# A two-layer trunk with a top-2-of-8 MoE: the last half in a fixed order, with a fourth pair of split buffers

## The chip, the cores and the metric

The kernel runs on one core of one Trainium2 chip. The metric is the device time of one execution in microseconds (us); it is compared as the median of several runs. The kernel before takes 1392.92 us (three runs, 1392.0 to 1393.23). Engines are called PE (TensorE, with its weight loads as PEld), DVE (VectorE), ACT (ScalarE), POOL (GpSimd) and SP (the engine that issues the DMAs).

## The reference

Input x has 256 tokens of 1024 values. There are two layers; each is a gated token mixer with four branches, then a feed-forward part: a dense SwiGLU in layer 0, a mixture of 8 SwiGLU experts in layer 1. The change lies in the experts alone:

```python
def swiglu(t, w1, w3, w2):
    return (jax.nn.silu(t @ w1) * (t @ w3)) @ w2

logits = t @ router
top_vals, top_idx = lax.top_k(logits, 2)
weights = jax.nn.softmax(top_vals, axis=-1)
combine = jnp.sum(jax.nn.one_hot(top_idx, 8) * weights[..., None], axis=1)
out = sum(combine[:, e:e + 1] * swiglu(t, w1[e], w3[e], w2[e]) for e in range(8))
```

Each expert has w1 and w3 of 1024 x 2816 and w2 of 2816 x 1024, all float32, 34.6 MB in sum. A final RMSNorm follows.

## The kernel before

**Precision.** A float32 matrix is split into two float32r parts: hi, a rounded copy made by ACT (`split_hi`, L132), and lo, the rest, made by DVE (`lo_parts`, L152). Products are summed in PSUM from hi x hi, lo x hi and hi x lo.

**The weight stream.** `plan` lists all weight tiles in the order of their use. A tile is 128 x 2048 float32, 1 MiB (the two last are half as large). `WeightStream` keeps three counters: tiles loaded, split hi, split lo. `SLOTS` names, for each phase of the plan, the SBUF slots that may hold a raw tile, a hi part or a lo part. `load` (L116, on SP) issues the next load once a raw slot is free, that is once DVE has made the lo part of the tile that was in it; `get` hands out a tile and splits ahead as far as slots are free.

**The experts.** The router's counts are ranked, and the four busiest experts get 128 slots each, the other four (`LIGHT`) 64 slots each (`Q`). An expert is worked through in six steps, chunks of 512 columns of the 2816 (the last has 256). A step of a full chunk uses two tiles of w1, two of w3, and two of w2 for the chunk before: six tiles. An expert has 33 tiles.

In the 64-slot half, the hi and lo part of the tokens stand side by side as 128 columns of one stationary operand, so that a weight tile costs eight matmuls of 512 columns: four with its hi part, then four with its lo part (`both`, L558). The banks of w1 and w3 are copied out by ACT (g and gb, L1314), the two halves of 64 are added by a short matmul with a folding matrix (L1352, `folded`), then ACT makes SiLU (L1355), DVE the product (L1356), ACT its hi part (L438) and DVE its lo part (L439). The result is the stationary operand of the w2 tiles, which are summed over the six chunks in two banks (yps). After an expert's last w2 tile these are weighted and split (y, L441 and L442), and after two experts matmuls with the slot masks (put) scatter them back to the tokens, which DVE adds to x (`scatter`, L1419 and L1420). The last expert's last chunk has its own function (`last_down`). Then the final norm is computed and written out.

**What sets the order.** The kernel is written in the order of the data. Where nothing else is said, a planner sets the order of each engine's instructions as it builds the program, by modelled times and free buffers. Some stretches (`manual_schedule`: the transitions between parts, and the routing) are in the order of the text; the loop over expert steps in `experts` is not one of them. Each engine, and SP's queue, carries out its instructions strictly in the order set.

Raw, hi and lo slots: while the first three steps with 64 slots per expert are used, 9 raw, 3 hi and 3 lo (phase moe2); then 11 raw (moe3), from step `M2` on 10 (moe and end), always with 3 hi and 3 lo.

Of the kernel before, what the change touches and what calls it, by code (L numbers as in the profile page):

```python
# [8 lines left out]
F32 = mybir.dt.float32  # L9
# [46 lines left out]
M0, M1, MQ, M2, END = 6, 11, 27, 40, 47  # L56
LIGHT, Q = 4, 64
FT = DFF // P
# [8 lines left out]
class WeightStream:  # L67
# [6 lines left out]
    def __init__(self, tc, plan, slots):  # L74
        self.tc, self.nc, self.plan, self.slots = tc, tc.nc, plan, slots
        self.gate = []
        self.pools, self.owner = {}, {}
        self.last_pair = {n: j for j, t in enumerate(plan) for kind in ("hi", "lo") for n in slots[t[-1]][kind]}
# [8 lines left out]
    def take(self, kind, j, dt):  # L87
        free = []
        for slot in self.slots[self.plan[j][-1]][kind]:
            if slot not in self.pools or (kind == "raw" and self.last_pair.get(slot, -1) >= self.nlo):  # L90
# [82 lines left out]
    def split_all(self, upto, parts):  # L173
        while self.nlo < min(upto, len(self.plan)):
            if not ((self.nhi > self.nlo or self.split_hi()) and self.split_lo(parts)):
                return

# [26 lines left out]
class Trunk:  # L204
# [56 lines left out]
    def plan(self):  # L261
# [19 lines left out]
        for l in self.layers:  # L281
# [27 lines left out]
            else:  # L309
                steps = [(e, c) for e in range(NE) for c in range(len(CHUNKS))]  # L310
                for s in range(len(steps) + 1):
                    phase = "late" if s == 0 else "moe0" if s < M0 else "moe1" if s < M1 else "moe2" if s < MQ else "moe3" if s < M2 else "moe" if s < END else "end"
# [21 lines left out]
    def spread_gain(self, src, row, out):  # L334

        nc = self.nc
        nc.vector.memset(row[0:1, D : D + P], 1.0)
        nc.sync.dma_start(row[0:1, :D], src[None, :])
        banks = [self.acc("gainps") for _ in range(2)]
        for c, ps in enumerate(banks):  # L340
            nc.tensor.matmul(ps, row[0:1, D : D + P], row[0:1, c * 512 : (c + 1) * 512], start=True, stop=True)
        for c, ps in enumerate(banks):
            nc.scalar.activation(out[:, c * 512 : (c + 1) * 512], ps, AF.Copy)
# [864 lines left out]
    def experts(self, l, ep, ap, xp, tok, cw, pos, pick, g0):  # L1208
# [51 lines left out]
        def place(pair):  # L1260

            ps = self.acc("putps")
            for j in range(2):
                for t in range(NT):
                    nc.tensor.transpose(
                        ps[:, j * T + t * P : j * T + (t + 1) * P], mask(t, pair, j).bitcast(F32), self.ident
                    )
            put = ep.tile([P, 2, T], F32R, tag="put", name="put")
# [3 lines left out]
        def weigh(pair):  # L1272

            ps = self.acc("wslps")
            for j in range(2):
                for t in range(NT):
                    nc.tensor.matmul(
                        ps[:, 2 * j : 2 * j + 2], mask(t, pair, j), cw2[:, t, 2 * pair + j, :], start=t == 0, stop=t == NT - 1
                    )
            nc.vector.tensor_reduce(  # L1280
# [3 lines left out]
        for s in range(1, len(steps)):  # L1284
            if s < len(steps):
                e, c = steps[s]
                c0, n = CHUNKS[c]
                nk = 2048 // n
                heavy = e < LIGHT
                xv = xe[e // 2] if heavy else xe["both"]  # L1290
                outs = []
                for nm in ("w1", "w3"):
                    ps = self.mm(nm)
                    nt = NK // nk
                    for k0 in range(nt):
                        w = ws.get((nm, l, e, c, k0))
                        if heavy:
                            self.prod(
                                ps[:, :n], lambda i, k: xv[i][:, k0 * nk + k, e % 2, :], lambda j, k: w[j][:, k, :],
                                range(nk), start=k0 == 0, stop=k0 == nt - 1,  # L1300
                            )
                        else:
                            self.both(
                                ps[:, :n], lambda k: xv[:, k0 * nk + k, e - LIGHT, :], lambda j, k: w[j][:, k, :],
                                range(nk), start=k0 == 0, stop=k0 == nt - 1,
                            )
                    outs.append(ps)
                if heavy:
                    g = self.gate(ep, *outs, n)
                else:  # L1310
                    sums = []
                    for ps, tag in zip(outs, ("g", "gb")):
                        half = ep.tile([P, 512], F32, tag=tag, name=tag)
                        nc.scalar.activation(half[:, :n], ps[:, :n], AF.Copy)  # L1314
                        sums.append(half)
            if len(done) == 2 or done and done[0][0] == NE - 2:
                self.scatter(done, put)
                done = []
            if s == M2 + 2:
                row = self.extra.tile([P, 2 * D], F32, tag="u", name="gain")  # L1320
                self.gain = row[:, D:]
                self.spread_gain(self.a["final_norm"], row, self.gain)
# [6 lines left out]
            if s < len(steps):  # L1329
                nf = n // P  # L1330
                ps = self.mm("actps")
                if heavy:
                    for f in range(nf):
                        nc.tensor.transpose(ps[:, f * P : (f + 1) * P], g[:, f * P : (f + 1) * P], self.ident)
                    act = act_pair()
                    self.hilo(*(x[:, :nf, :] for x in act), ps[:, :n].rearrange("p (f s) -> p f s", f=nf))
                else:
                    act = self.folded(ep, ap, ps, sums, nf)
                acts[s] = act
                if e in (1, 3) and c < 4:  # L1340
                    if c == 0:
                        pick = self.picks(ep, pos, e // 2 + 1)
                    gather(e // 2 + 1, c)
        self.last_down(l, acts, ys[NE - 1], wsl, put)

    def folded(self, ep, ap, ps, sums, nf):

        nc = self.nc
        for j, x in enumerate(sums):
            for f in range(nf):  # L1350
                o = j * T + f * Q
                nc.tensor.matmul(ps[:, o : o + Q], x[:, f * P : (f + 1) * P], self.fold, start=True, stop=True)  # L1352
        n = nf * Q
        g = ep.tile([P, T], F32, tag="gf", name="gf")
        nc.scalar.activation(g[:, :n], ps[:, :n], AF.Silu)  # L1355
        nc.vector.tensor_tensor(g[:, :n], ps[:, T : T + n], g[:, :n], op=ALU.mult)  # L1356
        act = ap.tile([P, 4, P], F32R, tag="ah", name="act", bufs=2)
        self.hilo(act[:, :nf, :Q], act[:, :nf, Q:], g[:, :n].rearrange("p (f s) -> p f s", f=nf))
        return act
# [50 lines left out]
    def scatter(self, done, put):  # L1410

        nc = self.nc
        for t in range(NT):
            for half in range(2):
                s = slice(half * 512, (half + 1) * 512)
                ps = self.acc("scps")
                parts = [(e, y) for e, pair in done for y in pair]
                for n, (e, y) in enumerate(parts):
                    nc.tensor.matmul(ps, put[:, e % 2, t * P : (t + 1) * P], y[:, s], start=n == 0, stop=n == len(parts) - 1)  # L1419
                nc.vector.tensor_tensor(self.x[t][:, s], self.x[t][:, s], ps, op=ALU.add)  # L1420
# [150 lines left out]
```

## Time and profile before

| | us |
|---|---|
| median of three runs | 1392.92 |
| the profiled execution | 1393.16 |
| its span, first to last instruction | 1391.2 |
| busy in the span: PE | 1315.8 |
| DVE | 1057.4 |
| ACT | 869.0 |
| HBM read | 384.99 MB, 277 GB/s over the span |

The span runs from the first to the last instruction on the core; the execution takes 1.96 us more. An engine's busy time is the time in which at least one of its instructions runs; matmuls are pipelined, so that a busy PE need not be at its peak. "DMA share" is the mean busy share of the 16 DMA engines. A wait is put down to what came last before the instruction started. The first 64-slot tile is used at about 1004 us.

### The profile page before, as it was taken

The page shows a single profiled execution, that of the slowest core. Times are in us where ns is not written, and L with a number is a line of the kernel's source. Part 1 is how long each engine was busy: PE and PEld are TensorE (multiplying, and loading weights), DVE is VectorE, ACT ScalarE, POOL GpSimd, SP SyncE. Part 2 cuts the span into 40 slices and gives each one's busy share as a digit, 9 for nine tenths or more (in the row PEclk, how much of TensorE's full clock was granted, in tenths as well). Part 3 has the DMA queues.
Part 4 walks back from the last instruction along what each step waited for, and adds up shares of the span by engine and source line. Part 5 has one row for each costly group of instructions (what it writes and reads, how often), then busy time and mean ns, then how long its engine had stood idle before and what let it go on. Part 6 is the DMA issues. An engine that isn't in the chain of part 4 may idle for free. (4 is left out here: it accounts for less than half of the span.)

```text
span 1391.2 us, 20094 instructions
## 1 busy us (share of the span) xinstructions
PE 1315.8 (95%) x8088; PEld 1149.6 (83%) x8088; DVE 1057.4 (76%) x874; ACT 869.0 (62%) x775; POOL 30.0 (2%) x52
## 2 busy tenths in 40 slices
PE   6999999999999999999999999999999888988885
PEld 6999999999989999978888888888877666666653
DVE  5976666554467766678888898888899888987986
ACT  5644445433455444457776776777788867777774
POOL 3110000000000000000000000000000000000000
PEclk9999999999999999999999999999999999999998
DMA  8746556565545676658989899999999999999980
GB/s 277 247 133 219 191 181 219 177 194 182 182 159 190 210 280 206 213 198 297 345 310 343 323 357 340 371 353 353 354 400 407 412 388 366 361 353 362 350 302 31
DMA packets 212127, 387.40 MB, mean 278 GB/s; under 512 B 7791, under 2 KB 98733, under 8 KB 212030
## 3 DMA queue, kind: packets, MB, share of 16 engines
q1 hardware_dynamic: 211214, 383.90, 77.6%
q0 software_dynamic: 816, 2.17, 0.5%
q8 instruction: 65, 1.06, 0.3%
q14 instruction: 32, 0.26, 0.0%
HBM read 384.99 MB, written 1.05 MB: 277 GB/s over the span
## 5 line engine op out<-in xcount | busy, mean ns | idle before, releaser
L152 DVE TENSOR_TENSOR J<-B,F 128x2048 fp32r<-128x2048 f32 x27 | 61.8, 2290 | 36.6 <-ACT F L132 35.4
L152 DVE TENSOR_TENSOR I<-A,E 128x2048 fp32r<-128x2048 f32 (+1 forms) x28 | 62.0, 2214 | 30.7 <-ACT E L132 30.7
L132 ACT ACTIVATE F<-B 128x2048 fp32r<-128x2048 f32 x27 | 51.7, 1913 | 39.0 <-PE mm L552 14.8
L839 ACT ACTIVATE sg<-mm,cols 128x256 f32<-128x256 f32 x64 | 26.8, 470 | 77.8 <-PE mm L552 49.7
L132 ACT ACTIVATE E<-A 128x2048 fp32r<-128x2048 f32 (+1 forms) x28 | 51.9, 1853 | 36.1 <-issue 12.6
L152 DVE TENSOR_TENSOR K<-C,G 128x2048 fp32r<-128x2048 f32 x25 | 57.2, 2290 | 16.8 <-ACT G L132 16.7
L152 DVE TENSOR_TENSOR L<-D,H 128x2048 fp32r<-128x2048 f32 x20 | 45.8, 2290 | 24.3 <-ACT H L132 24.3
L132 ACT ACTIVATE G<-C 128x2048 fp32r<-128x2048 f32 x25 | 47.8, 1913 | 25.5 <-issue 11.7
L558 PE MATMUL w<-I,xe 128*128 128x512 f32 (+1 forms) x176 | 47.6, 396 | 16.9 <-DVE I L152 16.9
L558 PEld LDWEIGHTS w<-I,xe 128*128 128x128 f32 x176 | 29.8, 195 | 29.7 <-DVE I L152 25.7
L132 ACT ACTIVATE H<-D 128x2048 fp32r<-128x2048 f32 x20 | 38.3, 1917 | 25.3 <-PE mm L552 11.1
L558 PE MATMUL w<-E,xe 128*128 128x512 f32 (+1 forms) x176 | 44.5, 378 | 0.7 <-ACT E L132 0.7
L152 DVE TENSOR_TENSOR K<-B,G 128x2048 fp32r<-128x2048 f32 (+1 forms) x17 | 35.7, 2102 | 8.5 <-ACT G L132 7.9
L845 DVE TENSOR_TENSOR sg<-pr,sg 128x512 f32<-128x512 f32 x24 | 16.6, 692 | 33.2 <-ACT sg L839 33.2
L450 POOL TENSOR_TENSOR rstd<-rstd,mhalf 128x1 f32<-128x1 f32 (+1 forms) x14 | 12.5, 895 | 1322.5 <-ACT fo L455 780.8
L152 DVE TENSOR_TENSOR J<-A,F 128x2048 fp32r<-128x2048 f32 (+1 forms) x17 | 35.6, 2100 | 6.2 <-ACT F L132 6.2
L558 PE MATMUL w<-J,xe 128*128 128x512 f32 (+1 forms) x128 | 32.7, 381 | 7.9 <-DVE J L152 7.8
L152 DVE TENSOR_TENSOR J<-t,F 128x2048 fp32r<-128x2048 f32 x15 | 34.4, 2290 | 7.2 <-ACT F L132 6.8
L152 DVE TENSOR_TENSOR K<-H,G 128x2048 fp32r<-128x2048 f32 x15 | 34.4, 2290 | 7.0 <-ACT G L132 6.9
L552 PE MATMUL w<-E,xe 128*128 128x512 f32 (+1 forms) x168 | 38.9, 372 | 0.0
L152 DVE TENSOR_TENSOR I<-s,E 128x2048 fp32r<-128x2048 f32 (+1 forms) x16 | 34.4, 2155 | 4.9 <-ACT E L132 4.8
L152 DVE TENSOR_TENSOR K<-D,G 128x2048 fp32r<-128x2048 f32 (+1 forms) x16 | 34.4, 2155 | 4.6 <-ACT G L132 4.6
(565 smaller groups left out, 3981.0 us busy)
## 6 DMA issues: line engine op xcount, KB each, us to landing
B<-in_moe_w_dram SPq DMA_DIRECT2D x26, 1024.0 KB, 6.5
C<-in_moe_w_dram SPq DMA_DIRECT2D x26, 1024.0 KB, 6.0
D<-in_moe_w_dram SPq DMA_DIRECT2D x26, 1024.0 KB, 6.4
s<-in_moe_w_dram SPq DMA_DIRECT2D x26, 1024.0 KB, 7.0
A<-in_moe_w_dram SPq DMA_DIRECT2D x25, 1024.0 KB, 6.8
H<-in_moe_w_dram SPq DMA_DIRECT2D x25, 1024.0 KB, 5.7
L<-in_moe_w_dram SPq DMA_DIRECT2D x25, 1024.0 KB, 5.9
t<-in_moe_w_dram SPq DMA_DIRECT2D x25, 1024.0 KB, 6.6
```

Of the source, the lines that this page charges most:

```text
L132: self.nc.scalar.activation(t[:, s], self.raw[j][:, s], AF.Copy)
L152: self.nc.vector.tensor_tensor(t[:, s], self.raw[j][:, s], self.hi[j][:, s].bitcast(F32), op=ALU.subtract)
L450: self.power = nc.gpsimd.tensor_tensor(r, t, self.mhalf[:, :n], op=ALU.pow)
L552: nc.tensor.matmul(ps, lhs(i, k), rhs(j, k), start=start and n == 0, stop=stop and n == len(steps) - 1)
L558: self.nc.tensor.matmul(ps, lhs(k), rhs(j, k), start=start and n == 0, stop=stop and n == len(steps) - 1)
L839: nc.scalar.activation(sg[:, s], psg[:, s], AF.Sigmoid, bias=self.col(l, "b_gate", i * 8 + 2 * j + c))
L845: nc.vector.tensor_tensor(sg, pr[j], sg, op=ALU.mult)
```

## The change

The phases of the 64-slot half get other slots: raw slots H and L become a fourth hi and a fourth lo slot. A slot may hold raw tiles until the plan needs it as part of a pair (`pair_due`). The loop over steps ends at the 128-slot half; the 64-slot half is a new function, `light`, which runs inside `manual_schedule` for ACT, DVE and PE. It walks through the tiles of the plan. For tile i it writes PE's matmuls, then PE's other work that is due, then the hi split of tile i+4, then ACT's other work that is due, then the lo split of tile i+2, then DVE's other work that is due. "Due" is given by `at(kind, j, f)`: f stands behind PE's tile j, behind the hi split of tile j, or behind the lo split of tile j. The work itself (copies, folds, SiLU, products, splits, scatters) is as before.

```diff
-    "moe3": {"raw": "ABCDHLstuyz", "hi": "EFG", "lo": "IJK"},
-    "end": {"raw": "ABCDHLstyz", "hi": "EFG", "lo": "IJK"},
-    "moe": {"raw": "ABCDHLstyz", "hi": "EFG", "lo": "IJK"},
+    "moe3": {"raw": "ABCDstu", "hi": "EFGH", "lo": "IJKL"},
+    "moe4": {"raw": "ABCDstuyz", "hi": "EFGH", "lo": "IJKL"},
+    "moe5": {"raw": "ABCDstyz", "hi": "EFGH", "lo": "IJKL"},
+    "end": {"raw": "ABCDstyz", "hi": "EFGH", "lo": "IJKL"},
...
-M0, M1, MQ, M2, END = 6, 11, 27, 40, 47
+M0, M1, ML, MQ, M2, END = 6, 11, 24, 27, 40, 47
+PHASES = ((1, "late"), (M0, "moe0"), (M1, "moe1"), (ML, "moe2"), (MQ, "moe3"), (M2, "moe4"), (END, "moe5"), (99, "end"))
+AHEAD_HI, AHEAD_LO = 4, 2
...
+    def pair_due(self, slot, j):
+        at = self.pair_at.get(slot, ())
+        n = bisect_left(at, self.nlo)
+        return n < len(at) and at[n] < j
...
+    def ahead(self, nhi, nlo):
+        while self.nhi < min(nhi, len(self.plan)):
+            assert self.split_hi()
+        while self.nlo < min(nlo, len(self.plan)):
+            assert self.split_lo()
...
+        ws.release()
+        with self.tc.manual_schedule(engines={ACT, DVE, PE}):
+            self.light(l, ep, ap, xe["both"], acts, ys, done, wsl, masks, place_parts)
+        self.last_down(l, acts, ys[NE - 1], wsl, masks["put"])
...
+        def up(i, w, nm, e, c, k0):
...
+            self.both(
+                ps[:, :n], lambda k: x4[:, k0 * nk + k, e - LIGHT, :], lambda j, k: w[j][:, k, :],
+                range(nk), start=k0 == 0, stop=last,
+            )
+            if nm == "w1" and k0 == 0:
+                if s % 12 == PLACE:
+                    turn, put, find, put_weights = place_parts(s // 12)
+                    at("mm", i + 1, turn)
+                    at("hi", i + 5, put)
+                    at("mm", i + 2, find)
+                    at("lo", i + 4, put_weights)
...
+            at("hi", i + 4, copy)
+            if nm == "w1":
+                return
...
+            if s == NE * len(CHUNKS) - 1:
+                for f in (fold, silu, mult, act_hi, act_lo):
+                    at("mm", i + 1, f)
+                return
+            at("mm", i + 2, fold)
+            at("hi", i + 6, silu)
+            at("lo", i + 4, mult)
+            at("hi", i + 7, act_hi)
+            at("lo", i + 5, act_lo)
+
+        def down(i, w, e, c, k0):
...
+            at("hi", i + 4, y_hi)
+            at("lo", i + 3, y_lo)
...
+            for t in range(NT):
+                at("mm", i + 3 + t, lambda t=t: scatter(t))
+                at("lo", i + 5 + t, lambda t=t: self.add_scattered(t, sums[t]))
+
+        first = ws.nuse
+        ws.ahead(first + AHEAD_HI, first + AHEAD_LO)
+        for i in range(first, len(ws.plan) - len(LAST)):
+            key, w = ws.hand_out()
+            if key[0] == "w2":
+                down(i, w, *key[2:])
+            else:
+                up(i, w, key[0], *key[2:])
+            ws.release()
+            run("mm", i)
+            ws.ahead(i + 1 + AHEAD_HI, 0)
+            run("hi", i + AHEAD_HI)
+            ws.ahead(0, i + 1 + AHEAD_LO)
+            run("lo", i + AHEAD_LO)
```

`copy`, `fold`, `silu`, `mult`, `act_hi`, `act_lo`, `y_hi`, `y_lo` and `scatter` hold one instruction, or one loop of them, of the list in the section before. The load of the final norm's gain and its spreading are cut in two in the same manner.

## Rows read from the trace of the kernel before

**Rows 1.** The page's sums: busy us (share of the span) and instructions per engine.

```profile
PE 1315.8 (95%) x8088; PEld 1149.6 (83%) x8088; DVE 1057.4 (76%) x874; ACT 869.0 (62%) x775; POOL 30.0 (2%) x52
```

**Rows 2.** Stretches: from:to, length, busy PE, PEld, DVE, ACT, POOL; clock, DMA share, GB/s.

```profile
650.00:1004.00 354.00, 354.00 (x1713) 296.31 (x1712) 310.13 (x186) 258.12 (x180) 0.00 (x0) 1.00 0.95 346
1004.00:1023.00 19.00, 19.00 (x94) 15.85 (x93) 18.96 (x12) 19.00 (x16) 0.00 (x0) 1.00 0.99 371
1020.00:1130.00 110.00, 97.90 (x481) 77.22 (x481) 99.18 (x66) 86.27 (x74) 0.00 (x0) 1.00 1.04 410
1130.00:1350.00 220.00, 188.31 (x888) 141.34 (x888) 187.37 (x119) 167.58 (x140) 0.00 (x0) 0.99 0.99 361
1004.00:1376.00 372.00, 324.33 (x1550) 248.68 (x1549) 322.94 (x213) 287.20 (x249) 0.00 (x0) 0.99 0.94 350
```

**Rows 3.** Waits of the engines, 1004 to 1376: us in total, times, longest us.

```profile
ACT g L1314 <- PE w L558: 27.5, 19, 2.0
...
DVE I L152 <- ACT E L132: 18.9, 15, 1.5
...
DVE I L152 <- DMA z<-in_moe_w_dram: 0.2, 1, 0.2
```

**Rows 4.** Order of time within 1150 to 1200: start, length, instruction [idle before, releaser].

```profile
1155.09 2.28 DVE L152 TENSOR_TENSOR J<-D,F 128x2048 fp32r<-128x2048 f32 x1
...
1155.92 1.08 PE L558 MATMUL w<-F,xe 128*128 128x512 f32 x4
1157.29 2.29 DVE L152 TENSOR_TENSOR K<-s,G 128x2048 fp32r<-128x2048 f32 x1
...
1158.66 0.60 ACT L1314 ACTIVATE g<-w 128x512 f32<-128x512 f32 x1 [1.96 <-PE w L558]
1159.15 1.90 ACT L132 ACTIVATE E<-A 128x2048 fp32r<-128x2048 f32 x1
...
1159.38 1.04 PE L1352 MATMUL actps<-fold,g 128*128 128x64 f32 x8
...
1161.09 2.29 DVE L152 TENSOR_TENSOR I<-A,E 128x2048 fp32r<-128x2048 f32 x1 [1.52 <-ACT E L132]
...
1163.44 1.19 PE L558 MATMUL w<-I,xe 128*128 128x512 f32 x4 [1.11 <-DVE I L152]
```

**Rows 5.** Waits of the DMA queue on SP, 1004 to 1376.

```profile
SPq L116 <- DVE gf L1356: 56.1, 20, 3.6
```

**Rows 6.** DMA, 1020 to 1130: packets, MB, share; issues, KB each, median us to landing.

```profile
q1 hardware_dynamic: 19829, 44.97, 104.1%
...
y<-in_moe_w_dram SPq DMA_DIRECT2D x4, 1024.0 KB, 11.4
z<-in_moe_w_dram SPq DMA_DIRECT2D x4, 1024.0 KB, 9.3
```

**Rows 7.** DMA, 1004 to 1376.

```profile
q1 hardware_dynamic: 58576, 130.00, 93.6%
...
B<-in_moe_w_dram SPq DMA_DIRECT2D x1, 512.0 KB, 4.7
```

**Rows 8.** Order of time at the end.

```profile
1346.64 0.38 SPq L116 DMA_DIRECT2D B<-in_moe_w_dram  x1
...
1364.68 0.39 ACT L1314 ACTIVATE gb<-w 128x256 f32<-128x256 f32 x1 [0.33 <-PE w L558]
...
1366.86 0.27 ACT L1355 ACTIVATE gf<-actps 128x128 f32<-128x128 f32 x1
...
1368.05 1.15 ACT L132 ACTIVATE G<-B 128x512 fp32r<-128x512 f32 x2
1368.32 0.28 DVE L1356 TENSOR_TENSOR gf<-actps,gf 128x128 f32<-128x128 f32 x1
...
1369.09 0.30 ACT L438 ACTIVATE act<-gf 128x128 fp32r<-128x128 f32 x1
...
1370.93 0.28 DVE L439 TENSOR_TENSOR act<-gf,act 128x128 fp32r<-128x128 f32 x1
```

More of the change, by code (lines that the diff above doesn't have):

```diff
@@ L1 @@
+from bisect import bisect_left
 from contextlib import ExitStack, contextmanager
@@ L77, in __init__ @@
         self.pools, self.owner = {}, {}
-        self.last_pair = {n: j for j, t in enumerate(plan) for kind in ("hi", "lo") for n in slots[t[-1]][kind]}
+        self.pair_at = {}
+        for j, t in enumerate(plan):
+            for n in slots[t[-1]]["hi"] + slots[t[-1]]["lo"]:
+                self.pair_at.setdefault(n, []).append(j)
         self.raw, self.hi, self.lo = {}, {}, {}
@@ L89, in take @@
         for slot in self.slots[self.plan[j][-1]][kind]:
-            if slot not in self.pools or (kind == "raw" and self.last_pair.get(slot, -1) >= self.nlo):
+            if slot not in self.pools or (kind == "raw" and self.pair_due(slot, j)):
                 continue
@@ L176, in split_all, with hand_out @@
                 return
+    def ahead(self, nhi, nlo):
[3 more added lines that the diff above has]
+            assert self.split_lo()
+    def hand_out(self):
+        i = self.nuse
+        assert self.nlo > i
+        key, _, k, c, _ = self.plan[i]
+        self.nuse += 1
+        return key, tuple(t.pop(i)[:, : k * c].rearrange("p (k c) -> p k c", k=k) for t in (self.hi, self.lo))
     def get_many(self, keys, ahead=True):
@@ L311, in plan @@
                 for s in range(len(steps) + 1):
-                    phase = "late" if s == 0 else "moe0" if s < M0 else "moe1" if s < M1 else "moe2" if s < MQ else "moe3" if s < M2 else "moe" if s < END else "end"
+                    phase = next(name for end, name in PHASES if s < end)
                     if s < len(steps):
@@ L332, in bcast, with load_row, spread_row, copy_row @@
         (eng or self.nc.gpsimd).dma_start(t, bass.AP(tensor=src.tensor, offset=src.offset, ap=[[0, P], [1, n]]))
[L334 to L338, printed above, removed]
+    def load_row(self, src, row):
+        self.nc.vector.memset(row[0:1, D : D + P], 1.0)
+        self.nc.sync.dma_start(row[0:1, :D], src[None, :])
+    def spread_row(self, row):
         banks = [self.acc("gainps") for _ in range(2)]
         for c, ps in enumerate(banks):
-            nc.tensor.matmul(ps, row[0:1, D : D + P], row[0:1, c * 512 : (c + 1) * 512], start=True, stop=True)
+            self.nc.tensor.matmul(ps, row[0:1, D : D + P], row[0:1, c * 512 : (c + 1) * 512], start=True, stop=True)
+        return banks
+    def copy_row(self, banks, out):
         for c, ps in enumerate(banks):
-            nc.scalar.activation(out[:, c * 512 : (c + 1) * 512], ps, AF.Copy)
+            self.nc.scalar.activation(out[:, c * 512 : (c + 1) * 512], ps, AF.Copy)
     def load_gain(self, src, eng=None):
@@ L1282, in weigh @@
             )
[L1284 to L1316, printed above, removed]
@@ new lines, in experts @@
+        for s in range(1, ML):
+            e, c = steps[s]
+            c0, n = CHUNKS[c]
+            nk = 2048 // n
+            xv = xe[e // 2]
+            outs = []
+            for nm in ("w1", "w3"):
+                ps = self.mm(nm)
+                nt = NK // nk
+                for k0 in range(nt):
+                    w = ws.get((nm, l, e, c, k0))
+                    self.prod(
+                        ps[:, :n], lambda i, k: xv[i][:, k0 * nk + k, e % 2, :], lambda j, k: w[j][:, k, :],
+                        range(nk), start=k0 == 0, stop=k0 == nt - 1,
+                    )
+                outs.append(ps)
+            g = self.gate(ep, *outs, n)
+            if len(done) == 2:
@@ L1317, in experts @@
                 self.scatter(done, put)
                 done = []
[L1319 to L1322, printed above, removed]
             if s % 12 == PLACE:
@@ L1328, in experts @@
                 done.append((steps[s - 1][0], y))
[L1329 to L1332, printed above, removed]
-                    for f in range(nf):
[L1334 to L1359, printed above, removed]
+            nf = n // P
@@ new lines, in experts @@
+            ps = self.mm("actps")
+            for f in range(nf):
+                nc.tensor.transpose(ps[:, f * P : (f + 1) * P], g[:, f * P : (f + 1) * P], self.ident)
+            act = act_pair()
+            self.hilo(*(x[:, :nf, :] for x in act), ps[:, :n].rearrange("p (f s) -> p f s", f=nf))
+            acts[s] = act
+            if e in (1, 3) and c < 4:
+                if c == 0:
+                    pick = self.picks(ep, pos, e // 2 + 1)
+                gather(e // 2 + 1, c)
+        masks = {"put": put}
@@ new lines, in place_parts, with put @@
+        def place_parts(pair):
+            def put():
+                masks["put"] = put_masks(masks["ps"])
+            return (
+                lambda: masks.update(ps=turn_masks(pair)), put,
+                lambda: masks.update(wps=find_weights(pair)), lambda: set_weights(pair, masks["wps"]),
+            )
+        ws.release()
+        with self.tc.manual_schedule(engines={ACT, DVE, PE}):
+            self.light(l, ep, ap, xe["both"], acts, ys, done, wsl, masks, place_parts)
+        self.last_down(l, acts, ys[NE - 1], wsl, masks["put"])
@@ new lines, in light, with at, run, copy @@
+    def light(self, l, ep, ap, x4, acts, ys, done, wsl, masks, place_parts):
+        nc, ws = self.nc, self.ws
+        todo = {"mm": [], "hi": [], "lo": []}
+        bank, half, now = {}, {}, [0]
+        def at(kind, j, f):
+            todo[kind].append((j, len(todo[kind]), f))
+        def run(kind, upto):
+            ready = sorted((x for x in todo[kind] if x[0] <= upto), key=lambda x: x[:2])
+            todo[kind] = [x for x in todo[kind] if x[0] > upto] if len(ready) < len(todo[kind]) else []
+            for _, _, f in ready:
+                f()
+        def up(i, w, nm, e, c, k0):
+            c0, n = CHUNKS[c]
+            nk, s = 2048 // n, e * len(CHUNKS) + c
+            if k0 == 0:
+                bank[nm] = self.mm(nm)
+            ps = bank[nm]
+            last = k0 == NK // nk - 1
+            self.both(
+                ps[:, :n], lambda k: x4[:, k0 * nk + k, e - LIGHT, :], lambda j, k: w[j][:, k, :],
+                range(nk), start=k0 == 0, stop=last,
+            )
+            if nm == "w1" and k0 == 0:
[5 more added lines that the diff above has]
+                    at("lo", i + 4, put_weights)
+                if s == M2 + 2:
+                    row = self.extra.tile([P, 2 * D], F32, tag="u", name="gain")
+                    self.gain = row[:, D:]
+                    banks = []
+                    self.load_row(self.a["final_norm"], row)
+                    at("mm", i + 6, lambda: banks.extend(self.spread_row(row)))
+                    at("hi", i + 10, lambda: self.copy_row(banks, self.gain))
+            if not last:
+                return
+            def copy():
+                half[nm] = ep.tile([P, 512], F32, tag={"w1": "g", "w3": "gb"}[nm], name="half")
+                nc.scalar.activation(half[nm][:, :n], ps[:, :n], AF.Copy)
+            at("hi", i + 4, copy)
+            if nm == "w1":
+                return
+            nf, box = n // P, {}
+            def fold():
+                box["ps"] = out = self.mm("actps")
+                for j, x in enumerate((half["w1"], half["w3"])):
+                    for f in range(nf):
+                        o = j * T + f * Q
+                        nc.tensor.matmul(out[:, o : o + Q], x[:, f * P : (f + 1) * P], self.fold, start=True, stop=True)
+            m = nf * Q
+            def silu():
+                box["g"] = ep.tile([P, T], F32, tag="gf", name="gf")
+                nc.scalar.activation(box["g"][:, :m], box["ps"][:, :m], AF.Silu)
+            def mult():
+                nc.vector.tensor_tensor(box["g"][:, :m], box["ps"][:, T : T + m], box["g"][:, :m], op=ALU.mult)
+            def act_hi():
+                acts[s] = act = ap.tile([P, 4, P], F32R, tag="ah", name="act", bufs=2)
+                nc.scalar.activation(act[:, :nf, :Q], box["g"][:, :m].rearrange("p (f s) -> p f s", f=nf), AF.Copy)
+            def act_lo():
+                act = acts[s]
+                nc.vector.tensor_tensor(
+                    act[:, :nf, Q:], box["g"][:, :m].rearrange("p (f s) -> p f s", f=nf), act[:, :nf, :Q].bitcast(F32),
+                    op=ALU.subtract,
+                )
+            if s == NE * len(CHUNKS) - 1:
+                for f in (fold, silu, mult, act_hi, act_lo):
+                    at("mm", i + 1, f)
+                return
+            at("mm", i + 2, fold)
[4 more added lines that the diff above has]
+        def down(i, w, e, c, k0):
+            if c == 0 and k0 == 0:
+                ys[e] = [self.acc("yps") for _ in range(2)]
+            y, act = ys[e], acts[e * len(CHUNKS) + c]
+            n = CHUNKS[c][1]
+            last = c == len(CHUNKS) - 1 and k0 == n // 256 - 1
+            for h in range(2):
+                self.down_part(
+                    e, y[h], act, k0, lambda j, k: w[j][:, k, h * 512 : (h + 1) * 512], c == 0 and k0 == 0, last,
+                )
+            if k0 == n // 256 - 1:
+                del acts[e * len(CHUNKS) + c]
+            if not last:
+                return
+            halves = [slice(h * 512, (h + 1) * 512) for h in range(2)]
+            weight = wsl[:, e : e + 1]
+            def y_hi():
+                pair = self.extra.tile([P, 2, D], F32R, tag="wx"[e % 2], name="y")
+                done.append((e, (pair[:, 0], pair[:, 1])))
+                for s, ps in zip(halves, y):
+                    nc.scalar.activation(pair[:, 0, s], ps, AF.Copy, scale=weight)
+            def y_lo():
+                hi, lo = done[-1][1]
+                for s, ps in zip(halves, y):
+                    nc.vector.scalar_tensor_tensor(
+                        lo[:, s], ps, weight, hi[:, s].bitcast(F32), op0=ALU.mult, op1=ALU.subtract
+                    )
+            at("hi", i + 4, y_hi)
+            at("lo", i + 3, y_lo)
+            if e % 2 == 0 and e < NE - 2:
+                return
+            sums = {}
+            def scatter(t):
+                sums[t] = self.scatter_half(done, masks["put"], t)
+                if t == NT - 1:
+                    done.clear()
+            for t in range(NT):
[15 more added lines that the diff above has]
+            run("lo", i + AHEAD_LO)
+        for kind in todo:
+            run(kind, 10**9)
@@ L1410, in scatter, with scatter_half, add_scattered @@
     def scatter(self, done, put):
-        nc = self.nc
         for t in range(NT):
[L1414 to L1420, printed above, removed]
+            self.add_scattered(t, self.scatter_half(done, put, t))
+    def scatter_half(self, done, put, t):
+        banks = []
+        for half in range(2):
+            s = slice(half * 512, (half + 1) * 512)
+            ps = self.acc("scps")
+            parts = [(e, y) for e, pair in done for y in pair]
+            for n, (e, y) in enumerate(parts):
+                self.nc.tensor.matmul(
+                    ps, put[:, e % 2, t * P : (t + 1) * P], y[:, s], start=n == 0, stop=n == len(parts) - 1
+                )
+            banks.append(ps)
+        return banks
+    def add_scattered(self, t, banks):
+        for half, ps in enumerate(banks):
+            s = slice(half * 512, (half + 1) * 512)
+            self.nc.vector.tensor_tensor(self.x[t][:, s], self.x[t][:, s], ps, op=ALU.add)
     def overflow(self, l, th, tl, cw, pos, cnti):
```

8 lines of the change are left out of this document (added).

## The prediction

> **What bounds the kernel now.** I read the sums of the page first, then the busy times by stage, then the waits of the last stage, then its instructions in order of time, then the DMA queue.
>
> The sums [rows 1] name no bound: TensorE (PE) 95%, VectorE (DVE) 76%. By stage [rows 2] there are two. From 650 to 1004 us, the experts with 128 slots, PE is busy 354.00 of 354.00 us: that half is bound by PE and the change doesn't touch it. From 1004 us on, the experts with 64 slots, no engine is full: over 1130:1350 PE has 188.31 of 220 us, DVE 187.37, ScalarE (ACT) 167.58, at 361 GB/s. One weight tile is 1 MiB (1.0486 MB), so 361 GB/s x 220 us is 79.4 MB or 75.7 tiles, and a tile takes 2.90 us, of which PE is busy 2.49, DVE 2.48, ACT 2.21. Busy counts the tails of waiting matmuls, so these are upper bounds of the work.
>
> Why a tile takes 2.90 us is in the waits [rows 3] and in the order of time [rows 4]. Nothing waits for data: DVE waited 0.2 us for a DMA, once. Instead the three engines wait for each other in a ring. At 1158.66 ACT copies a finished bank (g) after 1.96 us idle, because the bank needs PE's last matmuls; the hi split of the next tile (E from A) is queued behind that copy and starts at 1159.15; DVE's lo split of that tile waits for it, 1.52 us idle, to 1161.09; PE waits for that lo, 1.11 us idle, to 1163.44; and the next copy waits for PE. This happens at the g copy and at the gb copy, twice in every step of six tiles. With three hi and three lo buffers no engine is far enough ahead to cover it.
>
> The DMA queue follows this ring. SP waits for DVE to free a raw buffer, for some 260 us of 372 in five such lines, the longest of them in [rows 5]. Where more buffers were free, 1020:1130, the same loads ran at 410 GB/s with the 16 engines' packets at 104.1% of the time and 9.3 to 11.4 us from issue to landing [rows 2, 6]: by the rate 2.557 us a tile, so some four tiles in flight. That is the DMA's own limit as far as this trace shows it, and it lies above the 2.48 to 2.49 us of DVE and PE.
>
> **The change, part by part.**
> *Instructions.* None is added or removed: the same splits, matmuls, folds, copies and sums, in another order. Cost 0.
>
> *The fixed order.* The hi split of tile i+4 and the lo split of tile i+2 now stand ahead of PE's tile i+1, and each copy, SiLU and product stands behind a split that comes later. I followed one step through the order with DVE as the bound (DVE splits start 2.20 us apart, [rows 4]; PE 0.91 us for half a tile, estimated from its 1.08 us less the tail; ACT 1.90 a split). Say DVE ends the lo of the second tile after w3 at 0. PE ends that tile at 1.0 and the fold (16 short matmuls, 1.04 us for eight in [rows 4]) at about 2.9; ACT's SiLU ends at 3.3; DVE wants it at 4.4, after two more splits. The product ends at 4.8, ACT's next hi split (it needs PE's first half of the tile after the fold) at 5.7, act hi at 6.1; DVE wants it at 7.0. So both meeting points have about 1 us in hand, and the ring is gone. ACT needs 6 x 1.90 plus 2 us in a step of over 14. What is late next is the load: 2.557 us a tile against 2.48.
>
> *When the load is the bound*, ACT's hi split starts as a tile lands; the same order makes DVE wait for ACT to be two tiles ahead (product and act lo), so a raw buffer is freed up to some 7.5 us after landing (two tiles of 2.56, and a lo split). This costs nothing as long as enough loads are in flight.
>
> *Raw buffers.* Two become a hi and a lo slot: before 10 (11 and 9 at the edges), after 7 for the first three steps, then 9, then 8. A buffer's round is landing time plus the time it is held: 8 x 2.557 = 20.5 us, less 7.5 held, leaves 13 us, more than the 9.3 to 11.4 us that a saturated landing took [rows 6]. With 7 it leaves 10.4, just enough. Bounds: nothing, or the rate of a queue that runs shallow (346 GB/s over 650:1004, [rows 2]). I take the upper rate, 410, since the held time is nearer to that case. But two fewer tiles are in the buffers when the stage starts (7 for 9): 2 x 2.557 = +5.1 us; bounds 0 and 5.1.
>
> *The end.* Now the last load is issued at 1346.64 and lands 4.7 us later, at 1351.3 [rows 7, 8], 39.9 us before the end, because landed tiles are queued in the buffers. A stage bound by loads has no such queue. After the last landing comes its hi split 1.15, the copy behind it 0.39, fold (eight short matmuls) 1.04, SiLU 0.27, product 0.28, act hi 0.30, act lo 0.28 [rows 4, 8], six hand-overs at an estimated 0.15, together 4.6; from act lo's end (1371.2) to the end of the span are 20.0 us today; the last two lo splits now stand behind act lo, an estimated +0.4. Sum 25.0, bounds 22 and 39.9.
>
> *A rule against it.* In 1020:1130 the loads ran at 410 GB/s [rows 2, 6]. The Trainium skill, "DMA: Bandwidth & Descriptors", section "Where 436 GB/s comes from", says that for HBM to SBUF the limit of HBM per core, about 358 GB/s, binds. By it the loads could not speed up over today's 361, and the estimate of the stage would be 130.00 / 0.358 = 363 us. The trace disagrees for 110 us on end with one core running, but its last 220 us do stand near that figure, so it is a rival below.
>
> **The sum**, on the profiled execution:
> - start of the stage 1004, unchanged
> - loads left at 1004: 130.00 MB [rows 7]; the first 19 us as now, 371 GB/s [rows 2], 7.05 MB; the other 122.95 MB at 410 GB/s: 299.9 us; last landing 1322.9
> - two tiles less in the buffers: 1328.0
> - the end: 1353.0
> - for stalls I can't place (a scatter of 16 matmuls twice in the stage, seven buffers at its start) 1% of 300 us, my estimate: 1356.0, a span shorter by 35.2 us
> - outside the span 1393.16 - 1391.2 = 1.96; the median 1392.92 lies 0.24 under the profiled run: 1357.7.
>
> **The rivals.**
> 1. *Forecast*: loads bind, 1358 (own range 1350 to 1366). 0.62.
> 2. *The order stalls at places of its own.* In-order engines now have each small operation nailed behind a split; if the 1 us in hand is used up by hand-overs or by landings that vary, DVE's idle time comes back in part. It is 372 - 322.94 = 49 us now [rows 2]; half of it on top of the floor of rival 3: 1372. 0.17.
> 3. *Loads faster than I think, DVE binds.* DVE's busy time from 1004 to its act lo, 322.94 less some 2 us after it, ends at 1325; plus 20.0 and 1.7: 1347. Against it: 104.1% at 410 GB/s. 0.08.
> 4. *The loads stay at today's late rate*, 361 GB/s: 130.00 / 0.361 = 360.1 us from 1004; with or without the two tiles (5.8) and with the end of 25.0 and 1.7: 1391 to 1397. For it: packets already at 99% of the time over 1130:1350 [rows 2]. Against: SP waits for DVE there, and the same packets' share stood at 95% with 346. 0.06. By the skill's 358 it would be 1394 to 1400.
> 5. *Slower: too few raw buffers.* A buffer that is held longer than 20.5 - 10.4 = 10.1 us past its landing (7.5 in the first three steps) lets the queue run shallow. Place: every lo split that waits behind a product or act lo. Price: at the 346 GB/s of [rows 2], 130.00 / 0.346 = 375.7, two tiles 6.1, end 25.0, 1.7: 1412. Against it: my 7.5 us. 0.07.
>
> That the change doesn't do what it says I hold for excluded: nothing but the order and the slots is left to go wrong.
>
> **How the numbers follow.** About 0.2% (2.8 us) is what a measurement here tells from no change. Forecast and rivals 2 and 3 are faster: 0.87. Rival 4 is split, 0.03 the same and 0.03 slower; with rival 5 slower is 0.10. The range 1346 to 1378 holds the forecast, rival 3 and most of rival 2, about 0.83.
>
> **What would show it.** Right: SP no longer waits for DVE most of the time; DVE and ACT wait for DMA landings; about 405 to 415 GB/s from 1030 to 1320; the last landing near 1328 and 25 us to the end; ACT's idle time before the g and gb copies (27.5 us for g alone, [rows 3]) gone. Rival 2: DVE waits for ACT or PE with landed tiles in hand. Rival 3: over 420 GB/s. Rivals 4 and 5: waits for data at 346 to 361 GB/s, rival 4 with landings over 10 us, rival 5 with short landings and SP waiting for DVE before each issue. I am wrong in the first step if the half before 1004 us moves.

## The result, and the profile after

The changed kernel takes 1355.99 us (median of four runs, 1354.36 to 1356.61), the kernel before 1392.84 us beside it: a ratio of 0.9734, 95% interval 0.9718 to 0.9751. The forecast was 1357.7 us. The profiled execution is the shortest of the four, 1354.36 us with a span of 1352.7 us, 38.5 us less than before.

The stretches of the changed kernel come first: from:to, length, then busy PE, PEld, DVE, ACT, POOL; granted clock, DMA share, GB/s.

```profile
650.00:1004.00 354.00, 354.00 (x1714) 296.31 (x1713) 312.82 (x188) 261.14 (x182) 0.00 (x0) 1.00 0.94 340
1004.00:1023.00 19.00, 19.00 (x93) 15.87 (x92) 16.42 (x12) 17.56 (x16) 0.00 (x0) 1.00 1.05 408
1020.00:1130.00 110.00, 104.02 (x508) 84.07 (x507) 106.29 (x68) 94.72 (x78) 0.00 (x0) 0.97 1.04 409
1130.00:1310.00 180.00, 168.38 (x817) 132.90 (x815) 170.98 (x111) 155.27 (x129) 0.00 (x0) 0.99 1.05 410
1004.00:1337.00 333.00, 313.27 (x1535) 250.84 (x1533) 314.95 (x209) 284.22 (x245) 0.00 (x0) 0.98 1.01 396
```

Against [rows 2], the 128-slot half has the same busy PE, and the 64-slot half now moves 410 GB/s to its end, where it had fallen to 361. DVE went from 322.94 busy of 372 us (87%) to 314.95 of 333 (95%); the program gives it the same work, and its idle time in these stretches fell from 49 to 18 us.

The first 64-slot tile is used at 1001.80 us (1004.46 before). From there to the end of the span are 350.9 us, before 386.7: the stage gave 35.8 of the 38.5 us, and an earlier start of the stage 2.7. Over the eight profiled kernels of this document that first tile stands at 1001.8 to 1005.3 us, and the program's first transposes, which no run touches, at 8.1 to 9.4 us; so these 2.7 us can't be credited to the change.

The waits of the engines of the changed kernel in the same stage, 1004 to 1337: us in total, times, longest us.

```profile
DVE gf L1449 <- ACT gf L1446: 17.4, 11, 2.6
...
ACT gf L1446 <- PE actps L1440: 6.1, 11, 3.2
...
ACT F L145 <- DMA y<-in_moe_w_dram: 2.0, 3, 1.1
...
DVE act L1457 <- ACT act L1453: 0.5, 2, 0.4
```

The two links of the ring in [rows 3], ACT's g copy waiting for PE (27.5 us) and DVE's lo split waiting for ACT's hi split (18.9 us), have no row any more. DVE's largest wait is now for the SiLU, 17.4 us in 11 of 24 steps. ACT waits for landings 30 times, 14.8 us in sum; DVE for none.

The order of time of the changed kernel in one step, to lay beside [rows 4]:

```profile
1201.61 2.28 DVE L165 TENSOR_TENSOR L<-y,H 128x2048 fp32r<-128x2048 f32 x1
1201.61 0.58 ACT L1428 ACTIVATE half<-w 128x512 f32<-128x512 f32 x1
1202.08 1.92 ACT L145 ACTIVATE E<-A 128x2048 fp32r<-128x2048 f32 x1
...
1203.81 2.28 DVE L165 TENSOR_TENSOR J<-z,F 128x2048 fp32r<-128x2048 f32 x1
...
1206.01 2.28 DVE L165 TENSOR_TENSOR K<-s,G 128x2048 fp32r<-128x2048 f32 x1
...
1208.21 2.28 DVE L165 TENSOR_TENSOR I<-A,E 128x2048 fp32r<-128x2048 f32 x1
...
1209.84 1.89 PE L1440 MATMUL actps<-fold,half 128*128 128x64 f32 x16
...
1211.77 0.39 ACT L1446 ACTIVATE gf<-actps 128x256 f32<-128x256 f32 x1 [0.28 <-PE actps L1440]
...
1212.62 0.41 DVE L1449 TENSOR_TENSOR gf<-actps,gf 128x256 f32<-128x256 f32 x1
```

The copy at 1201.61 waits for nothing, and the hi split E behind it is done at 1204.0; DVE wants E at 1208.21, 4.2 us later. In [rows 4] the same lo split had waited 1.52 us for it. DVE starts its lo splits 2.20 us apart. The SiLU ends at 1212.16, 0.46 us before the product starts: this meeting point is the tight one.

The DMA of the changed kernel, 1004 to 1337: GB/s in 40 equal slices; packets, MB, share; issues, KB each, median us to landing.

```profile
GB/s 417 405 399 409 414 410 402 410 408 412 413 410 416 408 414 409 409 408 404 412 414 410 413 409 415 408 412 401 409 412 411 411 414 410 414 408 416 399 246 0
...
q1 hardware_dynamic: 59291, 131.43, 100.6%
...
t<-in_moe_w_dram SPq DMA_DIRECT2D x14, 1024.0 KB, 10.9
...
z<-in_moe_w_dram SPq DMA_DIRECT2D x14, 1024.0 KB, 15.0
...
A<-in_moe_w_dram SPq DMA_DIRECT2D x1, 512.0 KB, 10.5
```

The rate stands within 399 and 417 GB/s for 38 slices, 316 us. Landings took 10.9 to 15.0 us (medians by slot; before, in 1020:1130, they were 9.3 to 11.8, of which [rows 6] shows 11.4 and 9.3), by the rate more than four tiles in flight.

### The profile page after: what moved, and what is told of

Its sections match the earlier page's. It is cut to its first block, busy times and chain, and to the rows that moved or that the text cites. A ratio compares the mean times of both kernels' runs of the same rounds, so it can differ in the third digit from the quotient of the medians.

```text
span 1352.7 us, 20123 instructions
## 1 busy us (share of the span) xinstructions
PE 1308.0 (97%) x8088; PEld 1154.1 (85%) x8088; DVE 1055.1 (78%) x874; ACT 871.5 (64%) x775; POOL 29.2 (2%) x52
## 5 line engine op out<-in xcount | busy, mean ns | idle before, releaser
L165 DVE TENSOR_TENSOR J<-B,F 128x2048 fp32r<-128x2048 f32 (+1 forms) x33 | 72.2, 2189 | 36.6 <-ACT F L145 35.4
L145 ACT ACTIVATE F<-B 128x2048 fp32r<-128x2048 f32 (+1 forms) x33 | 60.6, 1838 | 41.0 <-PE mm L584 14.8
L165 DVE TENSOR_TENSOR L<-D,H 128x2048 fp32r<-128x2048 f32 (+1 forms) x29 | 64.1, 2213 | 24.3 <-ACT H L145 24.3
L145 ACT ACTIVATE H<-D 128x2048 fp32r<-128x2048 f32 (+1 forms) x29 | 53.8, 1857 | 28.6 <-PE mm L584 11.0
L1440 PEld LDWEIGHTS actps<-fold,half 128*128 128x128 f32 x352 | 43.0, 191 | 2.2
L1440 PE MATMUL actps<-fold,half 128*128 128x64 f32 x352 | 41.9, 271 | 0.0
L584 PE MATMUL w<-E,xe 128*128 128x512 f32 (+1 forms) x168 | 38.9, 372 | 0.0
L584 PE MATMUL mm<-hThi,F 128*128 128x256 f32 x256 | 35.9, 281 | 0.0
L584 PE MATMUL mm<-hThi,J 128*128 128x256 f32 x256 | 35.3, 279 | 0.0
L584 PE MATMUL mm<-hTlo,F 128*128 128x256 f32 x256 | 34.9, 278 | 0.0
## 6 DMA issues: line engine op xcount, KB each, us to landing
t<-in_moe_w_dram SPq DMA_DIRECT2D x28, 1024.0 KB, 10.4
```

Source lines behind the costliest of these rows:

```text
L145: self.nc.scalar.activation(t[:, s], self.raw[j][:, s], AF.Copy)
L165: self.nc.vector.tensor_tensor(t[:, s], self.raw[j][:, s], self.hi[j][:, s].bitcast(F32), op=ALU.subtract)
L584: nc.tensor.matmul(ps, lhs(i, k), rhs(j, k), start=start and n == 0, stop=stop and n == len(steps) - 1)
L1440: nc.tensor.matmul(out[:, o : o + Q], x[:, f * P : (f + 1) * P], self.fold, start=True, stop=True)
```

## The experiments

Two questions: is it the loads that set the new time, or DVE, which is 95% busy; and is it the order or the slots that broke the ring.

**Half of each load** (e1). Of each weight tile of the 64-slot half only the first half of the rows is loaded, and both splits read it twice; the output uses half of these weights.

```diff
+            if phase in HALF:
+                self.nc.sync.dma_start(t3[:, : k // 2, :], ap[:, : k // 2, :])
+                k = 0
...
+        return out.rearrange("p (r n) -> p r n", r=2), self.raw[j][:, None, :n].to_broadcast([P, 2, n])
```

> Each weight tile of the 64-slot half is loaded by half (0.5 MiB), and the hi and lo splits read that half twice, so that ScalarE, VectorE and TensorE do the same work on half of the weights. Theory L (the loads bind at 410 GB/s): the bound passes to VectorE, which had 18 us idle in the 333 us of the stage: 1338 to 1346 us, VectorE over 97% busy there, DMA at 205 to 220 GB/s. Theory O (the fixed order of the engines and VectorE bind, the 410 GB/s is only their demand): no change, 1353 to 1358 us, with VectorE waiting for ScalarE's SiLU as before (17 us).

Measured: 1342.12 us (1341.76 to 1343.03), ratio to the kernel before 0.9634 (0.9618 to 0.965). Its stretches, columns as above:

```profile
1004.00:1130.00 126.00, 121.46 (x603) 98.77 (x603) 123.41 (x80) 113.96 (x97) 0.00 (x0) 1.00 0.72 220
1130.00:1310.00 180.00, 174.16 (x855) 140.01 (x853) 179.34 (x116) 161.96 (x137) 0.00 (x0) 0.99 0.69 210
```

With half the bytes DVE is busy 179.34 of 180 us and the kernel is 13.9 us shorter. So the loads set the changed kernel's time, and the next bound, DVE, lies only 14 us below. DVE's wait for the SiLU, 17.4 us in the changed kernel, nearly goes too (1004 to 1376):

```profile
DVE gf L1465 <- ACT gf L1462: 3.7, 2, 2.6
```

**Half of each lo split** (e2). DVE makes the lo part of the first half of each such tile only, and PE uses it for both halves; the lo part of the second half is left out.

```diff
+        if phase in HALF:
+            n //= 2
...
+        return hi, Twice(lo, k) if phase in HALF else lo
```

> VectorE makes the lo part of only the first half of each weight tile of the 64-slot half, and TensorE reads that half twice; loads, ScalarE and TensorE are as in the changed kernel. Theory L: VectorE loses some 140 us of work and the time stays, 1350 to 1357 us (a little at the end, where lo splits stand behind the last load), with 405 to 412 GB/s. Theory O: the time falls by over 10 us, below 1346 us, and the loads run above 420 GB/s.

Measured: 1355.54 us (1353.6 to 1357.2), ratio 0.9726 (0.9706 to 0.9745). One stretch of it:

```profile
1130.00:1310.00 180.00, 167.52 (x821) 138.30 (x820) 99.84 (x110) 154.93 (x129) 0.00 (x0) 0.96 1.05 410
```

and its largest wait of DVE in the stage:

```profile
DVE gf L1465 <- ACT gf L1462: 96.1, 24, 5.5
```

DVE lost 71 of its 171 us in this stretch, and the time stayed: the rate is 410 again. Most of the freed time came back as wait for the SiLU, 96.1 us in all 24 steps. That row is a warning for the reader: the largest wait of this kernel, which is bound by loads, names the product and not the load. The landings are waited for further up the chain, at ACT's hi split (24.6 us in 53 waits, 1004 to 1337).

**The slots without the order** (e3). The kernel before with the new slots and phases; the planner still sets the order.

```diff
-    "moe3": {"raw": "ABCDHLstuyz", "hi": "EFG", "lo": "IJK"},
...
+    "moe3": {"raw": "ABCDstu", "hi": "EFGH", "lo": "IJKL"},
+    "moe4": {"raw": "ABCDstuyz", "hi": "EFGH", "lo": "IJKL"},
```

> The kernel before with the new slots alone (fourth hi and lo slot for raw slots H and L), in the planner's order. Theory A (the order is what ends the ring of waits): most of the ring stays, 1375 to 1393 us, VectorE waits for ScalarE's splits as before. Theory B (the fourth pair is what ends it): 1354 to 1366 us.

Measured: 1391.06 us (1389.93 to 1392.57), ratio 0.9981 (0.9968 to 0.9993). Its stretches:

```profile
1004.00:1130.00 126.00, 113.69 (x562) 90.92 (x561) 113.55 (x73) 100.60 (x86) 0.00 (x0) 1.00 1.04 410
1130.00:1310.00 180.00, 155.16 (x739) 116.41 (x738) 155.42 (x100) 138.71 (x117) 0.00 (x0) 1.00 0.98 360
```

and its waits, 1004 to 1376:

```profile
ACT g L1326 <- PE w L570: 30.0, 21, 2.0
ACT gb L1326 <- PE w L570: 28.0, 20, 2.1
DVE I L164 <- ACT E L144: 13.0, 9, 1.9
```

A fourth pair in place of two raw slots leaves the ring as it was: the g copy waits 30.0 us (27.5 in [rows 3]), DVE's lo splits wait 45.1 us for ACT's hi splits over all slots (before 44.7), and the late rate is 360 GB/s. With four pairs as with three, in the planner's order, a split waits behind a copy. The gain is 0.1 to 0.3%. More slots in all were not tried.

**The order without the slots** (e4). The changed kernel with the slots of before, three pairs and 9, 11, then 10 raw slots; hi splits run three tiles ahead instead of four, and ACT's other work moves up by one tile with them.

```diff
-AHEAD_HI, AHEAD_LO = 4, 2
+AHEAD_HI, AHEAD_LO = 3, 2
...
-            at("hi", i + 4, copy)
+            at("hi", i + 3, copy)
...
-            at("hi", i + 6, silu)
+            at("hi", i + 5, silu)
```

> The fixed order with three hi and three lo slots and the raw slots of before (9, 11, 10): the hi split of tile i+3 instead of i+4, and ScalarE's other work behind the split one tile earlier. Theory A (the order ends the ring, three pairs do, and the loads bind): two tiles more in the buffers at the start, 1349 to 1356 us, 410 GB/s. Theory B (the fourth pair is needed): over 1368 us, with VectorE waiting for ScalarE's splits and ScalarE for TensorE.

Measured: 1349.91 us (1349.15 to 1353.63), ratio 0.9686 (0.967 to 0.9702), which does not overlap that of the changed kernel: this version is faster than the one with both. Its stretches:

```profile
1004.00:1130.00 126.00, 121.46 (x604) 98.72 (x603) 125.58 (x80) 113.33 (x95) 0.00 (x0) 1.00 1.04 404
1130.00:1310.00 180.00, 171.54 (x833) 135.47 (x833) 174.07 (x112) 156.48 (x130) 0.00 (x0) 0.99 1.04 410
```

The same 410 GB/s with three pairs, and with ten raw slots for eight: so it is not the number of raw slots that holds the changed kernel at 410. In 1004:1130 DVE is busy 125.58 of 126 us, so DVE is the bound there, as long as landed tiles are queued. Its stage, from the first tile used (1005.21) to the end of its span (1351.9), takes 346.7 us against 350.9. The medians, each against the kernel before measured beside it: slots alone 1391.06 (-2.1 of 1393.20), order alone 1349.91 (-43.3 of 1393.20), both 1355.99 (-36.9 of 1392.84). On top of the order the fourth pair, paid for with two raw slots and run with the hi split one tile further ahead, costs some 6 us and buys nothing. In the profiled executions, e4's being the slowest of its four and the changed kernel's the fastest, the stage differs by 4.2 us; the forecast's term for two buffered tiles was 5.1.

**Fewer raw slots** (e5, e6). The changed kernel with six raw slots, then four, throughout the 64-slot half.

```diff
-    "moe4": {"raw": "ABCDstuyz", "hi": "EFGH", "lo": "IJKL"},
+    "moe4": {"raw": "ABCDst", "hi": "EFGH", "lo": "IJKL"},
```

> The changed kernel with six raw slots in the whole 64-slot half (A, B, C, D, s, t) instead of 7, 9 and 8. Rule of the buffer's round: 6 x 2.557 = 15.3 us, less 7.5 us held after landing, leaves 7.8 us to land, three loads in flight. If three in flight keep the 410 GB/s: 1356 to 1361 us (one tile less in the buffers at the start is 2.6 us). If the queue runs shallow at three (theory of rival 5: 346 to 361 GB/s): 1390 to 1412 us.

Measured: 1368.92 us (1367.68 to 1369.5), ratio 0.9824 (0.9808 to 0.9841). This lies between what the two theories expected, a miss for both. A stretch of it:

```profile
1130.00:1310.00 180.00, 166.32 (x803) 129.46 (x804) 165.87 (x106) 150.86 (x124) 0.00 (x0) 0.99 1.03 394
```

and its DMA, 1004 to 1320, where the mean was 392 GB/s:

```profile
DMA packets 55426, 124.02 MB, mean 392 GB/s; under 512 B 1887, under 2 KB 8031, under 8 KB 55407
...
C<-in_moe_w_dram SPq DMA_DIRECT2D x20, 1024.0 KB, 8.0
```

The rate over the same 316 us, in 40 slices of 7.9 us, tells what the mean hides:

```profile
GB/s 409 369 318 326 382 402 408 406 408 407 413 407 415 388 383 379 377 393 407 410 400 414 410 412 375 345 345 415 409 411 404 408 412 410 413 398 337 361 408 408
```

In 25 slices the loads run at 400 to 415 GB/s, so six slots mostly do; over 1222:1278 the mean is 410 with median landings of 7.6 to 9.0 us, that is 3.0 to 3.5 tiles in flight. The other 15 slices come in four groups, and each group begins within a slice of an expert's y split on DVE (1018.2, 1105.5, 1192.6, 1280.2). At the second of these DVE waits 1.46 us for the SiLU, then makes a product and the y split ahead of its next lo split, and two loads go out 5.5 us apart (1103.74, 1109.23). By 410 GB/s the 15 slices fall short by some 13 us of loading, about the size of the loss (12.9 us). So three tiles in flight did keep the 410 GB/s, as the first theory had it, except behind the end of an expert, which neither theory had priced.

As a mean, a tile takes 2.675 us at 392 GB/s, six of them 16.05 us; less 8.0 us to landing, a buffer was held 8.0 us past it (the forecast's estimate: 7.5).

> The changed kernel with four raw slots in the whole 64-slot half (A, B, C, D). The shortest landing seen is 4.7 to 5.2 us and a slot is held 4.2 (its hi and lo split) to 7.5 us, so a tile takes 9.4 / 4 = 2.35 to 12.7 / 4 = 3.2 us; with 2.557 as the floor and three tiles less at the start (7.7 us): 1362 to 1445 us, most likely some 1400, with SyncE waiting for VectorE before nearly every load, 320 to 390 GB/s, and VectorE and ScalarE waiting for landings. If the fixed order were what binds, and not the loads, it would stay below 1362 us.

Measured: 1447.95 us (1444.9 to 1448.87), ratio 1.0387 (1.0367 to 1.0407): slower than the kernel before, and above the 1362 to 1445 us that were expected. A stretch of it:

```profile
1130.00:1310.00 180.00, 143.82 (x625) 113.08 (x626) 137.15 (x84) 121.57 (x98) 0.00 (x0) 0.89 0.89 323
```

its engines' waits and SP's, 1004 to 1320:

```profile
ACT H L145 <- DMA C<-in_moe_w_dram: 28.8, 21, 4.9
```

```profile
SPq L129 <- DVE L L165: 66.9, 24, 8.1
```

and its DMA in the same stretch:

```profile
DMA packets 46481, 102.89 MB, mean 326 GB/s; under 512 B 1569, under 2 KB 7713, under 8 KB 46464
...
A<-in_moe_w_dram SPq DMA_DIRECT2D x25, 1024.0 KB, 5.4
...
D<-in_moe_w_dram SPq DMA_DIRECT2D x24, 1024.0 KB, 6.1
```

Short landings, waits for data and SP waiting for DVE before nearly every issue: the signs that the forecast had named for rival 5. So that mechanism is real, and seven to nine slots keep the kernel clear of it. The expectation took 4.7 to 5.2 us to landing, and 5.4 to 6.1 were measured. PE's granted clock was lower too in this stretch (0.89 against 0.99); what that adds to the time no run here separates.

## Why the prediction was right

**The ring and the order.** Right, and shown: the g copy's wait is gone with the order (e4) and not with the slots (e3). The hand-made walk through one step found both meeting points about 1 us in hand; at the SiLU the trace shows 0.46 us in the step above and 17.4 us of waits in all. With half the bytes they fell to 3.7 us (e1), so they come with the loads as bound and are no stall of the order's own. What no run separates is which part of the order ends the ring: the splits ahead of the small operations, or how far ahead they stand; three tiles ahead do as well as four (e4).

**Loads as the next bound.** Right: 410 GB/s to the end, e1 faster and e2 not. The Trainium skill bears on this place twice. "DMA: Bandwidth & Descriptors", section "Where 436 GB/s comes from", states without a condition that the HBM limit, about 358 GB/s per core, binds such loads; the trace disagrees with 399 to 417 GB/s for 316 us. The Trainium skill, "Perfetto Trace Analysis", section "Roofline", says that a core that is alone active in its pair can pull more than that share, with about 120% as the practical ceiling; 410 is 115% of 358, and the trace agrees.

**The sum, term by term.**
- Start 1004, unchanged: 2.7 us too late, of which 1.3 us is there already at the program's first transposes (8.1 against 9.4 us), ahead of anything that the change touches in the 64-slot half. By the spread over the eight profiled kernels this is luck.
- The first 19 us at 371 GB/s: they ran at 408, worth 1.7 us.
- Two tiles less in the buffers: 131.43 MB were loaded after 1004 instead of 130.00, 1.4 tiles more where the forecast took 2. The earlier start may hide a part of the rest.
- 410 GB/s for the rest: measured 409 to 410.
- Last landing 1328.0. The last order of time, of the changed kernel's end:

```profile
1315.57 0.37 SPq L129 DMA_DIRECT2D A<-in_moe_w_dram  x1
...
1317.16 0.38 SPq L129 DMA_DIRECT2D B<-in_moe_w_dram  x1
...
1328.75 1.15 ACT L145 ACTIVATE F<-B 128x512 fp32r<-128x512 f32 x2
...
1330.35 0.72 PE L590 MATMUL yps<-G,act 128*128 128x512 f32 x2 [1.58 <-DVE act L1457]
...
1332.31 1.00 PE L1440 MATMUL actps<-fold,half 128*128 128x64 f32 x8
1333.35 0.28 ACT L1446 ACTIVATE gf<-actps 128x128 f32<-128x128 f32 x1 [3.18 <-PE actps L1440]
...
1334.33 0.29 DVE L1457 TENSOR_TENSOR act<-gf,act 128x128 fp32r<-128x128 f32 x1 [0.38 <-ACT act L1453]
```

  A's half tile landed 10.5 us after its issue, at 1326.1. The view has no landing for B, but the core's DMA moves 94 GB/s in 1326:1327 and nothing in 1327:1328, so B was in by about 1326.9, 1.1 us earlier than forecast.
- The end, 25.0: 1352.7 - 1326.9 = 25.8. The size is right and two parts in it are off against each other. From the landing to the end of act lo (1334.6) are 7.7 us, not 4.6, because the fold stood on PE behind a w2 tile that waited for DVE (1330.35); from there to the end 18.1 instead of 20.4.
- The allowance of 3 us for stalls: without it the sum gives a span of 1353.0, and 1352.7 was measured. But that is with the start 2.7 us early. From the start of the stage the sum gives 349.0 us without the allowance and 352.0 with it, and 350.9 were measured, so about 2 of the 3 us were used.
- Landings when the queue is full, taken as 9.3 to 11.4 us: the view behind [rows 6] goes up to 11.8 (slot D), which stays under the 13 us that the forecast had for eight slots but not under the 10.4 us for seven. The first 19 us and 1020:1130 still ran at 408 and 409 GB/s.

**The signs.** Two were mis-sized. SP was to stop waiting for DVE most of the time: its rows for DVE, lo splits above all, still make up 166 of 333 us (before, counted in the same way, 276 of 372). These are the two largest rows of SP's queue in the changed kernel, against 56.1 us in [rows 5]:

```profile
SPq L129 <- DVE K L165: 38.2, 20, 3.7
SPq L129 <- DVE J L165: 37.1, 23, 3.7
```

A raw slot is reloaded as soon as it is free, so SP waits for one whether the loads bind or not; the time to landing tells the two apart, not this wait. And the waits for landings come to only 14.8 us. That fits two bounds that lie 14 us apart (e1; by the forecast DVE needs 2.48 of the 2.56 us that a tile takes), and the sign should have been priced at about that.

**The rivals.** Order stalls (1372) and loads at 361 GB/s (1391) did not come. DVE as bound was priced at 1347; e1 shows 1342. Too few raw slots, the one on the slower side, was rightly given a low chance: at seven to nine slots it does not decide, at six it costs 13 us, at four 92. Its place, lo splits behind a product, shows in e5 where a y split comes on top. Its deciding point was put at a hold of 10.1 us, and the holds worked out from e5 and e6 are 8.0 and (4 x 3.22 us at 326 GB/s, less some 5.7) 7.2.

**Left open.** Why the planner's order ran at 410 GB/s in its first 126 us (e3 shows it again) before the ring closed was not settled. In that stretch of the kernel before the g copy waits 4.5 us, in the 126 us after it 13.8 us. DVE makes 48 lo splits in it, one in 2.63 us, which is the pace of the loads there (404 GB/s, 2.60 us a tile), and 78 from 1130 to 1350, one in 2.82 us. So the ring costs little at first and the loads can be the bound there already; what lets it close later is open, and the landed tiles held at the start are a reason that was only argued.

## What to carry to other kernels

When no engine is full, look in the order of time for a ring of short waits between in-order queues: a fourth pair of split buffers in place of raw ones gave 0.1 to 0.3% here, a fixed order that puts the long split ahead of the small waiting operation took 3%. Once the ring is gone, price the next bound by its own best stretch in the trace, and count what the buffers hold at the start of the stage: here the fourth pair, for which two raw slots were given away, returned less than it cost. Size raw buffers by a round: buffers times the time per tile must cover landing plus hold, and the hold to reckon with is that of the worst place (here the end of an expert), not the mean. Look at the rate by slice before you read a bend into a mean.

## What the runs showed of the hardware

- Loads in flight, as landing time over time per tile of 1 MiB: 10.9 to 15.0 us at 409 to 410 GB/s (4.3 to 5.9 tiles, changed kernel); 7.6 to 9.0 us at 410 (3.0 to 3.5 tiles, e5 over 1222:1278); 5.4 to 6.1 us at a mean of 326 (about 1.8 tiles, e6). So some three tiles in flight kept the rate here, and with about 1.8 it fell.
- 410 GB/s held for 316 us on one core, and half as many bytes (e1) left the splits' durations as they were, 2.28 us a lo split on DVE and 1.90 to 1.92 us a hi split on ACT: the loads did not slow them.
